# Zero rows below the low part of the filter states, so that the tap matmuls all have 128 rows

## The chip, the cores and the metric

The kernel runs on one core of one Trainium2 chip. The time is device microseconds of one execution; the number compared is the median over several executions. Lower is better.

## What is computed

One layer of a bidirectional encoder with 1024 tokens and 1024 channels in float32: an RMS norm, one input projection, a Hyena branch (512 channels, two long convolutions with implicit filters) beside windowed attention (8 heads), gates, norms, and an output projection with a residual. What matters here is how the filters come about and what they are used for:

```python
def hyena_filters(L, w1, b1, w2, b2, w3, b3, w4, sin_freq):
...
    h = jnp.sin(fr * (z @ w1.astype(F32) + b1.astype(F32)))
    h = jnp.sin(fr * (h @ w2.astype(F32) + b2.astype(F32)))
    h = jnp.sin(fr * (h @ w3.astype(F32) + b3.astype(F32)))
    h = (h @ w4.astype(F32)).reshape(L, HYENA_ORDER, N_DIRS, D_HYENA)
...
    return h * decay[:, None, None, :]

def long_conv(u, k_f, bias):
    L = u.shape[1]
    y = jnp.fft.irfft(jnp.fft.rfft(u, n=2 * L, axis=1) * k_f[None], n=2 * L, axis=1)[:, :L]
    return y + u * bias
```

The states h before w4 have 64 values for each of the 1024 positions (FILTER_HIDDEN is 64). The matmul with w4 makes the filter taps.

## The kernel before

All large matmuls run on float32 values that were split into a high part, rounded to the matmul's input type (F32R), and a low part, the rest. A product takes the terms high x high, high x low and low x high.

*The projection* goes through 26 column tiles of 128 channels. `weights` (L164 on) loads a tile by the SP queue into `wraw`, writes the high part on ACT, the negated high part in float32 on ACT into the low tile, and adds the raw weights onto it by a DMA of the POOL queue (L177). `half` (L192 on) makes the matmuls L198 to L200 with 512 columns each; `qkv_half` makes L285 to L287 with 256 columns.

*The Hyena branch* works on four quarters of 128 channels. A quarter has two long convolutions (`long_conv`: transform by matmuls L531, butterflies and products on VectorE, inverse transform by matmuls L570, product with a gate on VectorE, L571). Each needs the spectrum of its filter, made by `filter_spectrum`, eight calls in all. A call makes the taps in 8 chunks of 128 positions, two chunks to a PSUM bank: for each chunk L402 multiplies the high states `hh` with the weights, and L403 adds the low states `hl`. VectorE multiplies a bank with the decay (L404) into `eo`, and the transform matmuls L416 read `eo`. So there are 8 x 8 = 64 matmuls L402 and as many L403.

*How the taps' three terms fit two matmuls.* The contraction has only 64 values. `filter_weights` therefore stacks the weights in `wf`: rows 0 to 63 hold the high part, rows 64 to 127 the low part (L383, L384). `filter_mlp` writes the high states into both halves of `hh` (L359). One matmul of 128 rows, L402, gives high x high and high x low. L403 gives low x high with 64 rows, and its tile `hl` has 64 partitions (L354, written by L361).

*What sets the order.* The instructions are ordered when the program is built: `weave` runs the Hyena branch and the projection side by side, by costs that the generators yield, and a scheduler puts each engine's instructions into one order. TensorE thus works through taps, transforms and projections in a fixed sequence. Three PSUM banks (NF) serve the taps, the transforms and the inverse transforms.

Of the kernel before, what the change touches and what calls it, by code (L numbers as in the profile page):

```python
# [9 lines left out]
F32 = mybir.dt.float32  # L10
F32R = mybir.dt.float32r
I32 = mybir.dt.int32
AF = mybir.ActivationFunctionType
ALU = mybir.AluOpType
# [4 lines left out]
P = 128  # L19
S = 1024  # L20
# [24 lines left out]
def view(ap, off, dims):  # L45
    return bass.AP(
        tensor=ap.tensor, offset=ap.offset + off, ap=[list(ap.ap[0])] + [list(d) for d in dims]
    )


class Kernel:
# [268 lines left out]
    def filter_mlp(self, mp, keep, ps):  # L320
        nc, a = self.nc, self.a
        pk = mp.tile([P, 904], F32, name="mlp_in")
        nc.sync.dma_start(pk[:, 0:904], a["mlp_in"])
        yield
        zT, w1, fb = pk[0:66, 0:512], pk[0:66, 512:640], pk[:, 896:900]
        w23 = pk[:, 640:896].rearrange("p (l c) -> p l c", l=2)
        V = nc.vector
        h = None
        for l in range(3):
            pt = ps.tile([P, 512], F32, tag="g", name=self.nm("mlp"))  # L330
            if l == 0:
                nc.tensor.matmul(pt, w1, zT, start=True, stop=True)
            else:
                nc.tensor.matmul(pt, w23[:, l - 1, :], h, start=True, stop=True)
            y = mp.tile([P, 512], F32, tag="my", name=self.nm("my"))
            k = mp.tile([P, 512], F32, tag="mk", name=self.nm("mk"))
            V.tensor_scalar(
                out=y, in0=pt, scalar1=fb[:, l : l + 1], scalar2=fb[:, 3:4], op0=ALU.add, op1=ALU.mult
            )
            V.tensor_scalar(  # L340
                out=k, in0=y, scalar1=1.0 / (2.0 * math.pi), scalar2=MAGIC, op0=ALU.mult, op1=ALU.add
            )
            V.tensor_scalar(out=k, in0=k, scalar1=-MAGIC, scalar2=None, op0=ALU.add)
            V.scalar_tensor_tensor(out=y, in0=k, scalar=-TWO_PI_A, in1=y, op0=ALU.mult, op1=ALU.add)
            V.scalar_tensor_tensor(out=y, in0=k, scalar=-TWO_PI_B, in1=y, op0=ALU.mult, op1=ALU.add)
            V.tensor_scalar(
                out=y, in0=y, scalar1=3.1415925, scalar2=-3.1415925, op0=ALU.min, op1=ALU.max
            )
            h = mp.tile([P, 512], F32, tag="mh", name=self.nm("mh"), bufs=2)
            nc.scalar.activation(h, y, AF.Sin)  # L350
            yield

        hh = keep.tile([P, S], F32R, name="hh")
        hl = keep.tile([64, S], F32R, name="hl")  # L354
        self.hh, self.hl = hh, hl
        for n in range(2):
            cols, src = slice(512 * n, 512 * n + 512), h[64 * n : 64 * n + 64]
            for k in range(2):
                nc.scalar.copy(hh[64 * k : 64 * k + 64, cols], src)  # L359
            own = hh[64 * n : 64 * n + 64, cols]  # L360
            V.tensor_tensor(out=hl[:, cols], in0=src, in1=own.bitcast(F32), op=ALU.subtract)  # L361
        self.h3 = h

    def filter_weights(self, o, mp, keep, ps):
# [21 lines left out]
    def filter_spectrum(self, o, s, fp, ps):  # L386
        nc = self.nc
        V = nc.vector
        ADD, SUB = ALU.add, ALU.subtract
        if (o, s) == (0, 0):  # L390
            dec = self.dec0
        else:
            dec = self.dp.tile([P, 8, CH], F32, tag="dec", name=self.nm("dec"), bufs=1)
            nc.sync.dma_start(dec, self.a["decay"][s])
        eo = fp.tile([P, 8, 2, CH], F32, tag="eo", name=self.nm("eo"), bufs=1)
        wf = self.wf[:, o, s].rearrange("p e c -> p (e c)")
        for t in range(0, 8, 2):
            pt = ps.tile([P, 2, 2, CH], F32, tag="f", name=self.nm("gen"))
            for k in range(2):
                pf = pt[:, k].rearrange("p e c -> p (e c)")  # L400
                cols = slice((t + k) * P, (t + k + 1) * P)
                nc.tensor.matmul(pf, self.hh[:, cols], wf, start=True, stop=False)  # L402
                nc.tensor.matmul(pf, self.hl[:, cols], wf[0:64], start=False, stop=True)  # L403
            V.tensor_tensor(  # L404
                out=eo[:, t : t + 2], in0=pt, in1=view(dec[:, t], 0, [[CH, 2], [0, 2], [1, CH]]), op=ALU.mult
            )
            yield 1.1
        V.tensor_copy(eo[0:1, 0, 0, :], self.e0[32 * o : 32 * o + 1, s * CH : (s + 1) * CH])

        pos, neg = self.d, self.dn

        def dft(out, terms):
            for n, (m, t, e) in enumerate(terms):
                nc.tensor.matmul(out, m, eo[:, t, e], start=n == 0, stop=n == len(terms) - 1)  # L416

        def x_part(out, t):
            if t in (0, 4):
                dft(out[:, 0], [(pos[:, t, 0], t, 0)])  # L420
                dft(out[:, 1], [(pos[:, t, 1], t, 1)])
            else:
                dft(out[:, 0], [(pos[:, t, 0], t, 0), (pos[:, 8 - t, 0], 8 - t, 0)])
                dft(out[:, 1], [(pos[:, t, 1], t, 1), (pos[:, 8 - t, 1], 8 - t, 1)])

        def y_part(out, t):
            dft(out[:, 0], [(pos[:, t, 1], t, 0), (neg[:, 2 + t, :], 8 - t, 0)])
            dft(out[:, 1], [(neg[:, t - 1, :], t, 1), (pos[:, 8 - t, 0], 8 - t, 1)])

        def bank(a, b):  # L430
            pt = ps.tile([P, 2, 2, CH], F32, tag="f", name=self.nm("dft"))
            for k, (f, t) in enumerate((a, b)):
                f(pt[:, k], t)
            return pt

        def tmp(tag, n=2):
            return fp.tile([P, n, 2, CH], F32, tag=tag, name=self.nm(tag), bufs=1)

        def copied(pt):
            t = fp.tile([P, 2, 2, CH], F32, tag="c0", name=self.nm("fc"), bufs=2)  # L440
            nc.scalar.copy(t, pt)
            return t

        def tt(out, x, y, op):
            V.tensor_tensor(out=out, in0=x, in1=y, op=op)

        kt = fp.tile([P, 8, 2, CH], F32, tag="kt", name=self.nm("kt"), bufs=1)

        def two(q, r):
            return view(kt[:], q * 2 * CH, [[(r - q) * 2 * CH, 2], [1, 2 * CH]])  # L450

        flat = [[1, 2 * CH]]
        tq = tmp("t")
        x04 = copied(bank((x_part, 0), (x_part, 4)))
        tt(tq[:, 0], x04[:, 0], x04[:, 1], ADD)
        tt(tq[:, 1], x04[:, 0], x04[:, 1], SUB)
        xy2 = bank((x_part, 2), (y_part, 2))
        gh = fp.tile([P, 2, 2, 2, CH], F32, tag="b4", name=self.nm("gh"))
        tt(gh[:, 0], tq, xy2, ADD)
        tt(gh[:, 1], tq, xy2, SUB)  # L460
        yield 2.4
        xy1 = copied(bank((x_part, 1), (y_part, 1)))

        xy3 = bank((x_part, 3), (y_part, 3))
        uv = fp.tile([P, 2, 2, 2, CH], F32, tag="b4", name=self.nm("uv"))
        tt(uv[:, 0], xy1, xy3, ADD)
        tt(uv[:, 1], xy1, xy3, SUB)
        yield 1.4
        W = 2 * CH
        g01 = view(gh[:], 0, [[2 * W, 2]] + flat)  # L470
        h01 = view(gh[:], W, [[2 * W, 2]] + flat)
        uv0 = view(uv[:], 0, [[3 * W, 2]] + flat)
        tt(two(0, 2), g01, uv0, ADD)
        tt(two(4, 6), g01, uv0, SUB)
        uw = tmp("t")
        tt(uw[:, 0], uv[:, 1, 0], uv[:, 0, 1], ADD)
        tt(uw[:, 1], uv[:, 1, 0], uv[:, 0, 1], SUB)
        uwf = view(uw[:], 0, [[W, 2]] + flat)
        for q, r, c in ((1, 7, RT), (5, 3, -RT)):
            V.scalar_tensor_tensor(out=two(q, r), in0=uwf, scalar=c, in1=h01, op0=ALU.mult, op1=ADD)  # L480
        yield 3.2
        return kt
# [695 lines left out]
```

## Time and profile before

| | |
|---|---|
| median of 3 runs | 709.48 us (707.67 to 712.77) |
| the profiled execution | 707.97 us, its span 706.2 us |
| TensorE matmul busy | 660.3 us (94%) |
| VectorE busy | 527.4 us (75%) |
| ScalarE busy | 288.1 us (41%) |
| POOL busy | 56.5 us (8%) |
| mean granted TensorE clock | 0.978 |

Names in the profile: PE is TensorE's matmul, PEld its weight load, which runs beside matmuls, DVE is VectorE, ACT is ScalarE, POOL is GpSimd. A row such as `L403 PE MATMUL gen<-wf,hl 64*128 64x256 f32` tells the line, the engine, the output and inputs by tile names (buffer numbers left out), the loaded weights (rows * columns) and the moving operand (rows x columns). In rows in order of time the first number is the start in us from the start of the span, the second the length. Matmuls are pipelined: the start of the next one comes before the end of the last, and the distance between starts tells how long one holds the engine.

### The profile page before, as it was taken

To read this page: it belongs to the slowest core of one execution; us is meant where nothing else is said; L and a number is where in the kernel's file an instruction comes from. 1 tells how busy PE (TensorE), PEld (TensorE's weight loads), DVE (VectorE), ACT (ScalarE), POOL (GpSimd) and SP (SyncE) were. 2 spreads that over 40 slices of the span, in tenths; PEclk is the share of its full clock that TensorE was granted. 3 is DMA by queue.
4 is the path that set the end of the run, shared out by engine and by line. 5 is a ranking of instruction groups with operands and counts; after the bars stand their busy time and mean duration, and the time that the engine had idled before them with its cause. 6 is when DMAs were issued, how large, how long until landed. Compare 5 with 4: busy or idle time off the path is not lost.

```text
span 706.2 us, 10609 instructions
## 1 busy us (share of the span) xinstructions
PE 660.3 (94%) x3962; PEld 569.9 (81%) x3962; DVE 527.4 (75%) x1161; ACT 288.1 (41%) x549; POOL 56.5 (8%) x64
## 2 busy tenths in 40 slices
PE   1489999999799999999999999999899899999997
PEld 1357788998788999888889888778787788988886
DVE  3878699598696998978979869444688878876422
ACT  6455343225242322432332423587377634343210
POOL 1341000001010000110100101010000000000000
PEclk9989999999999999999999999999899789999999
DMA  8934644235544313762450546754434731222331
GB/s 281 255 90 90 194 107 102 91 74 135 169 113 127 73 47 135 174 138 77 115 184 31 117 138 149 221 157 120 134 130 128 262 123 59 97 91 98 111 107 59
DMA packets 46888, 90.13 MB, mean 128 GB/s; under 512 B 7154, under 2 KB 15986, under 8 KB 46580
## 3 DMA queue, kind: packets, MB, share of 16 engines
q1 hardware_dynamic: 36656, 73.22, 31.3%
q0 software_dynamic: 7488, 13.63, 11.3%
q10 hardware_dynamic: 2692, 2.60, 1.3%
q8 instruction: 31, 0.51, 0.3%
q14 instruction: 21, 0.17, 0.1%
HBM read 53.78 MB, written 22.02 MB: 107 GB/s over the span
## 4 chain that ended last, share of the span: by engine, by line
PE 80%; DMA 13%; DVE 3%; ACT 2%; issue 2%; SPq 0%; ACTq 0%; DVEq 0%; POOLq 0%
PE proj L198 9%; PE proj L200 9%; PE proj L199 8%; PE pv L757 5%; PE dft L416 5%; PE fw L531 4%; PE inv L570 4%; PE po L844 4%; PE po L845 4%; PE po L846 4%; PE qkv L287 3%; PE qkv L285 3%; PE qkv L286 3%; DMA w_lo<-wraw 3%; PE gen L403 3%; PE gen L402 2%
## 5 line engine op out<-in xcount | busy, mean ns | idle before, releaser
L199 PE MATMUL proj<-h,w_hi 128*128 128x512 f32 x320 | 130.1, 407 | 1.8 <-DVE h L160 1.2
L198 PE MATMUL proj<-h,w_hi 128*128 128x512 f32 x320 | 129.1, 404 | 2.8 <-ACT h L158 2.8
L200 PE MATMUL proj<-h,w_lo 128*128 128x512 f32 x320 | 128.3, 401 | 0.0
L177 POOL DMA_DIRECT2D w_lo<-wraw x52 | 45.0, 866 | 418.8 <-ACT w_lo L176 383.4
L199 PEld LDWEIGHTS proj<-h,w_hi 128*128 128x128 f32 x320 | 61.1, 191 | 17.1 <-DVE h L160 2.4
L198 PEld LDWEIGHTS proj<-h,w_hi 128*128 128x128 f32 x320 | 61.2, 192 | 15.3 <-ACT h L158 3.6
L200 PEld LDWEIGHTS proj<-h,w_lo 128*128 128x128 f32 x320 | 61.3, 191 | 13.4 <-issue 1.3
L174 ACT CAST w_hi<-wraw 128x512 fp32r<-128x512 f32 x52 | 32.2, 620 | 76.1 <-DMA wraw<-in_w_in 39.6
L287 PE MATMUL qkv<-w_hi,h 128*128 128x256 f32 x192 | 54.9, 286 | 0.0
L285 PE MATMUL qkv<-w_hi,h 128*128 128x256 f32 x192 | 54.8, 286 | 0.0
L286 PE MATMUL qkv<-w_lo,h 128*128 128x256 f32 x192 | 54.8, 286 | 0.0
L757 PEld LDWEIGHTS pv<-vv,pf 128*128 128x128 f32 x352 | 49.5, 205 | 2.4 <-PE bT L719 0.2
L757 PE MATMUL pv<-vv,pf 128*128 128x66 f32 x352 | 48.7, 282 | 0.0
L416 PE MATMUL dft<-eo,d 128*128 128x128 f32 x352 | 46.8, 276 | 0.0
L416 PEld LDWEIGHTS dft<-eo,d 128*128 128x128 f32 x352 | 43.4, 192 | 0.6
L706 DVE CUSTOM_DVE_ANT_0 mj<-smax,mask 128x384 f32<-128x384 f32 (+1 forms) x64 | 33.4, 522 | 13.9 <-PE smax L701 10.8
L287 PEld LDWEIGHTS qkv<-w_hi,h 128*128 128x128 f32 x192 | 36.9, 192 | 0.5
L286 PEld LDWEIGHTS qkv<-w_lo,h 128*128 128x128 f32 x192 | 36.9, 192 | 0.2
L285 PEld LDWEIGHTS qkv<-w_hi,h 128*128 128x128 f32 x192 | 36.9, 192 | 0.3
L176 ACT ACTIVATE w_lo<-wraw 128x512 fp32r<-128x512 f32 x52 | 32.7, 629 | 10.5 <-PE qkv L286 10.5
L743 ACT ACTIVATE pf<-st 128x768 f32<-128x768 f32 (+1 forms) x32 | 24.2, 756 | 29.6 <-DVE st L741 26.8
L531 PE MATMUL fw<-u,d 128*128 128x128 f32 x256 | 33.4, 285 | 2.4 <-DMA u<-hy 2.3
(196 smaller groups left out, 1439.7 us busy)
## 6 DMA issues: line engine op xcount, KB each, us to landing
wraw<-in_w_in SPq DMA_DIRECT2D x52, 256.0 KB, 3.0
w_lo<-wraw POOLq DMA_DIRECT2D x52, 256.0 KB, 3.6
hy<-hraw SPq DMA_DIRECT2D x12, 512.0 KB, 2.6
x<-in_x_t SPq DMA_DIRECT2D x8, 512.0 KB, 5.4
dec<-in_decay SPq DMA_DIRECT2D x8, 512.0 KB, 3.9
g<-hy SPq DMA_DIRECT2D x8, 512.0 KB, 3.9
gt<-graw SPq DMA_DIRECT2D x16, 256.0 KB, 3.7
woraw<-in_w_out SPq DMA_DIRECT2D x16, 256.0 KB, 3.2
```

The source lines that it names most:

```text
L176: nc.scalar.mul(l, raw, -1.0)
L177: nc.gpsimd.dma_start(l.bitcast(F32), raw, accum_op=ALU.add)
L198: nc.tensor.matmul(pt, hi[:, k], xh, start=k == 0, stop=False)
L199: nc.tensor.matmul(pt, hi[:, k], xl, start=False, stop=False)
L200: nc.tensor.matmul(pt, lo[:, k], xh, start=False, stop=k == 7)
L285: nc.tensor.matmul(pt[:, b], hh, hi[:, :, k], start=k == 0, stop=False)
L286: nc.tensor.matmul(pt[:, b], hh, lo[:, :, k], start=False, stop=False)
L287: nc.tensor.matmul(pt[:, b], hl, hi[:, :, k], start=False, stop=k == 7)
L416: nc.tensor.matmul(out, m, eo[:, t, e], start=n == 0, stop=n == len(terms) - 1)
L531: nc.tensor.matmul(pt[:, k, c], self.d[:, t + k, c], u[:, t + k], start=True, stop=True)
L706: V.tensor_tensor_reduce(out=junk[:, 0:nk], in0=pm[:, 0:nk], in1=mask, op0=ALU.add, op1=ALU.max, scale=1.0, scalar=NEG, accum_out=mx[:, 4 ...
L757: nc.tensor.matmul(pv[:, h], probs[:, n, cols], self.vv[:, k0 + n, g], start=n == 0, stop=n == nk - 1)
```

## The change

The tile `hl` gets 128 partitions. Its partitions 64 to 127 are set to zero once, on GpSimd, and the low states are written into partitions 0 to 63, as before. L403 (L404 in the changed kernel) then reads all 128 rows of `hl` and all 128 rows of `wf`. What it adds is the same: the low states meet the high weights, and the zeros meet the low weights. In the matmul, `hl` is the operand that is loaded, `wf` the one that moves.

```diff
         hh = keep.tile([P, S], F32R, name="hh")
-        hl = keep.tile([64, S], F32R, name="hl")
+        hl = keep.tile([P, S], F32R, name="hl")
+        nc.gpsimd.memset(hl[64:128].bitcast(F32), 0.0)
         self.hh, self.hl = hh, hl
...
-            V.tensor_tensor(out=hl[:, cols], in0=src, in1=own.bitcast(F32), op=ALU.subtract)
+            V.tensor_tensor(out=hl[0:64, cols], in0=src, in1=own.bitcast(F32), op=ALU.subtract)
...
                 nc.tensor.matmul(pf, self.hh[:, cols], wf, start=True, stop=False)
-                nc.tensor.matmul(pf, self.hl[:, cols], wf[0:64], start=False, stop=True)
+                nc.tensor.matmul(pf, self.hl[:, cols], wf, start=False, stop=True)
```

The order of TensorE, VectorE, ScalarE and SP stays the same, instruction by instruction. POOL gets one more. This is the head of POOL's order before (the four constants are the program's own, `w_lo` the low weights of the projection, `wraw` what was loaded for them):

```order
L1168 MEMSET const-float32-0.0 128x1
L1168 MEMSET const-float32-1.0 128x1
L1168 MEMSET const-bfloat16-1.0 128x1
L1168 MEMSET const-uint8-127 128x1
L1174 UNCONDITIONAL_BRANCH
L177 DMA w_lo<-wraw_150 128x512
L177 DMA w_lo<-wraw_155 128x512
```

And the same place now:

```order
L1169 MEMSET const-float32-0.0 128x1
L1169 MEMSET const-float32-1.0 128x1
L1169 MEMSET const-bfloat16-1.0 128x1
L1169 MEMSET const-uint8-127 128x1
L1175 UNCONDITIONAL_BRANCH
L355 MEMSET hl 64x1024
L177 DMA w_lo<-wraw_150 128x512
L177 DMA w_lo<-wraw_155 128x512
```

The memset stands ahead of POOL's first DMA for the projection's weights; the rest of POOL's order follows as before.

On TensorE this is how taps stand among projections (here the first chunks of the second spectrum, `gen`, with the inverse transform of the convolution before, `inv`, ahead of them and the projection `qkv` behind). Before:

```order
L570 MATMUL inv_742<-V_713,di 128x128 x2
L402 MATMUL gen_755<-wf,hh 128x256
L403 MATMUL gen_755<-wf,hl 128x256
L402 MATMUL gen_755<-wf,hh 128x256
L403 MATMUL gen_755<-wf,hl 128x256
L287 MATMUL qkv_1163<-w_hi,h_89 128x256
```

And now, one line number further on:

```order
L571 MATMUL inv_743<-V_714,di 128x128 x2
L403 MATMUL gen_756<-wf,hh 128x256
L404 MATMUL gen_756<-wf,hl 128x256
L403 MATMUL gen_756<-wf,hh 128x256
L404 MATMUL gen_756<-wf,hl 128x256
L287 MATMUL qkv_1164<-w_hi,h_89 128x256
```

Nothing moved there; the rows tell the size of the output, which is the same, and not the rows of the operands, which are what changes.

## What I predicted, before the changed kernel ran

> **What bounds the kernel now.** I read the page first, for the chain that ended last, then the waits of TensorE and VectorE in the stretch where filter taps are made, then single rows there.
>
> From the page: the profiled span, and the chain by engine.
>
> ```profile
> span 706.2 us, 10609 instructions
> PE 80%; DMA 13%; DVE 3%; ACT 2%; issue 2%; SPq 0%; ACTq 0%; DVEq 0%; POOLq 0%
> ```
>
> The taps are made between 68 and 412 us. First TensorE's waits between 66 and 455 us (total, times, longest), then VectorE's waits between 114 and 412 us, where seven of the eight spectra lie, and the busy time of that stretch (length, then PE, PEld, DVE, ACT, POOL, the granted clock, the DMA share).
>
> ```profile
> PE uT L230 <- DVE hsc L220: 3.9, 1, 3.9
> PE fw L531 <- DMA u<-hy: 2.3, 2, 1.5
> DVE eo L404 <- PE gen L403: 13.2, 18, 1.6
> DVE u L571 <- PE inv L570: 7.0, 7, 1.8
> 114.00:412.00 298.00, 292.59 (x1911) 260.12 (x1911) 251.87 (x439) 95.71 (x190) 24.81 (x29) 0.99 0.42 115
> ```
>
> TensorE waits three times in 389 us, 6.2 us in all. It sets the pace here, and what leaves it can leave the time. But VectorE is busy 251.87 of 298 us (85%), so it comes next: 46 us of slack. The two of its waits that lie among the taps are for the taps themselves (13.2) and for the inverse transform that runs between them (7.0).
>
> **What a 64-row matmul costs.** The groups by shape (mean ns of one last before the bar; matmuls overlap, so a mean is no cost), then TensorE in order of time: one pair of tap chunks among projections, two neighbours of an earlier one, plain 256-column matmuls, and the 66-row matmuls of the attention.
>
> ```profile
> L403 PE MATMUL gen<-wf,hl 64*128 64x256 f32 x64 | 23.9, 378 | 0.0
> L286 PE MATMUL qkv<-w_lo,h 128*128 128x256 f32 x192 | 54.8, 286 | 0.0
> L736 PE MATMUL st<-qb,kt 66*128 66x256 f32 x88 | 25.0, 304 | 0.8 <-ACT qb L721 0.8
> ...
> 77.44 0.39 PE L200 MATMUL proj<-h,w_lo 128*128 128x512 f32 x1
> 77.67 0.28 PE L402 MATMUL gen<-wf,hh 128*128 128x256 f32 x1
> 77.88 0.38 PE L403 MATMUL gen<-wf,hl 64*128 64x256 f32 x1
> 78.19 0.38 PE L402 MATMUL gen<-wf,hh 128*128 128x256 f32 x1
> 78.50 0.38 PE L403 MATMUL gen<-wf,hl 64*128 64x256 f32 x1
> 78.81 0.50 PE L198 MATMUL proj<-h,w_hi 128*128 128x512 f32 x1
> 79.15 0.39 PE L199 MATMUL proj<-h,w_hi 128*128 128x512 f32 x1
> ...
> 68.57 0.50 PE L403 MATMUL gen<-wf,hl 64*128 64x256 f32 x2
> ...
> 113.94 0.28 PE L285 MATMUL qkv<-w_hi,h 128*128 128x256 f32 x1
> 114.06 0.28 PE L286 MATMUL qkv<-w_lo,h 128*128 128x256 f32 x1
> 114.17 0.28 PE L287 MATMUL qkv<-w_hi,h 128*128 128x256 f32 x1
> ...
> 476.53 0.29 PE L736 MATMUL st<-qb,kt 66*128 66x256 f32 x1
> 476.65 0.28 PE L735 MATMUL st<-qa,kt 128*128 128x256 f32 x1
> 476.77 0.28 PE L736 MATMUL st<-qb,kt 66*128 66x256 f32 x1
> ```
>
> Read the distances between starts. Plain 256-column matmuls follow each other in 0.12 us. L402 to L403 and back takes 0.31, and the 512-column L198 behind the last L403 takes 0.34. Without a 64-row neighbour a 512-column one takes 77.67 - 77.44 = 0.23. Each matmul loads its own weights, so a new load alone is not what costs: the plain ones load too. Nor is it short rows as such: 66 rows and 128 rows alternate in the attention at 0.12. What is left is the change between a 64-row and a 128-row shape, either way.
>
> From 77.44 to 79.15 are 1.71 us; two matmuls of 512 columns and four of 256 at the plain pace are 2 x 0.23 + 4 x 0.12 = 0.94. The excess is 0.77 for two L403, thus 0.385 each, two switches of 0.19.
>
> **The change part by part.**
>
> *The matmuls.* All 64 L403 become 128-row matmuls of the same 256 columns, and nothing else on TensorE changes. Price of one afterwards: at best the 0.12 of L286, at worst what it is now (0.31). I take 0.12, since L286 has the very shape (128*128, 256 columns) and L402, its neighbour, already has it. That a product with zeros is slower no row suggests. The gain on TensorE is 64 x 0.385 = 24.6, less four switches (0.8) in the first spectrum, where two L403 stand together (the x2 row at 68.57, and one more such pair) and share them: 24 us (3.4% of the span).
>
> The Trainium skill ("TensorE: Matmul & The Clock Gate", Part 3, The mechanism) says that weight loads overlap matmuls in flight only when their row groups differ. By that rule a 128-row load behind a 128-row matmul could not overlap, and the gain would be nil, a time of 708. The rows at 113.94 to 114.17 speak against it.
>
> *The larger tile.* The tile has 4 KB in a partition as before. L361 writes the same 64 rows.
>
> *The memset.* It is POOL's first work. Its price lies between the kernel's 128x1 memset and twice POOL's 128x512 subtraction (1024 elements a partition instead of 512).
>
> ```profile
> 0.24 0.10 POOL L1168 MEMSET const-float32-0.0<- 128x1 f32 x1 [0.24 <-issue]
> 11.99 1.90 POOL L177 DMA_DIRECT2D w_lo<-wraw  x2 [11.54 <-ACT w_lo L176]
> 28.15 1.39 POOL L160 TENSOR_TENSOR h<-x,h 128x512 fp32r<-128x512 f32 x1
> ```
>
> That is 0.1 to 2.8 us, and I take 2.8, the nearer size. POOL is idle for 11.54 us before its first DMA, so it costs nothing on the path; without that cover it would delay the w_lo DMA by those 2.8. The first reader, L403, comes at 68.57. No other engine waits for it before.
>
> **How much of the 24 us arrives.** *First spectrum (66 to 87).* The chain leaves TensorE here (start, length; the row at 369.89 is for the clock, below), and one VectorE row shows what stands before e0p:
>
> ```profile
> 73.24 0.95 PE e0p L378 x2
> 75.97 7.09 DMA hy<-hraw
> 83.14 3.52 DMA u<-hy
> 86.79 1.14 PE fw L531 x8
> ...
> 369.89 2.47 PE fw L531 x20
> ...
> 71.92 1.28 DVE L382 TENSOR_TENSOR wd<-w 64x512 f32<-64x512 f32 x2 [2.07 <-DMA w<-in_filt_w]
> ```
>
> Eight L403 save 8 x 0.385 - 0.8 = 2.3 us there, 0.8 of it at 77.44, after the store of hy began. The second e0p needs the weights whose landing released L382 at 71.92, so it can move from 73.2 by about 1.2 at most. I take 1.2 (ends 0 and 2.3). The rest becomes a longer wait for u, which is late next.
>
> *The seven others.* On TensorE each has 8 L403 x 0.385 = 3.08 us. The next transform needs the taps after VectorE's multiplication with the decay, so a spectrum cannot shrink by more than VectorE's own waits in it. Those are 13.2 + 7.0 = 20.2 us over the seven. In two of them they are more than TensorE can give (the seventh, then the eighth):
>
> ```profile
> DVE eo L404 <- PE gen L403: 2.4, 2, 1.6
> DVE u L571 <- PE inv L570: 1.6, 1, 1.6
> ...
> DVE u L571 <- PE inv L570: 2.4, 2, 1.8
> DVE eo L404 <- PE gen L403: 1.5, 3, 0.6
> ```
>
> 4.0 and 3.9 count as 3.08 each, so 20.2 - 0.9 - 0.8 = 18.5 us. The remaining 3 us of TensorE's gain turn into short waits for eo in front of the transforms. The ends are 10 (only half comes through, since VectorE is 85% busy and a late eo delays the next step) and 21.6 (7 x 3.08).
>
> *The clock.* After TensorE's longest wait (3.9 us, for hsc) the granted clock fell. After the 1.5 us wait for u, which ended at 369.89, it did not. Later there was a stretch at half (500 to 505).
>
> ```profile
> 184.10:188.00 3.90, 3.88 (x20) 3.90 (x21) 3.28 (x7) 1.17 (x2) 0.00 (x0) 0.56 0.08 24
> 369.90:374.00 4.10, 4.10 (x37) 4.10 (x38) 3.28 (x8) 1.48 (x3) 0.00 (x0) 1.00 0.01 5
> 500.00:505.00 5.00, 5.00 (x21) 4.44 (x21) 4.54 (x6) 4.13 (x5) 0.00 (x0) 0.50 0.13 52
> ```
>
> Such a stretch costs 3.9 x 0.44 = 1.7 us. The two waits for u, at 86.79 (2.3 - 1.5 = 0.8 us now) and at 369.89, may reach 2 us. I take 1.0 for both together (ends 0 and 3.4).
>
> *Sum.* -1.2 - 18.5 + 1.0 = -18.7. The profiled execution took 707.97 us, its span and 1.8 around it, so 689.3. The median before is 709.48, 1.5 above that execution; for a median I put half of that on top: 690.
>
> **Rivals.**
> 1. *All of it arrives*: TensorE is the only bound, and VectorE's work moves into its 46 us of slack. 708 - 24 = 684. For it: three waits in 389 us. Against it: 85% busy, and the single eo waits are smaller than what TensorE saves.
> 2. *VectorE takes the pace*: only half of the seven spectra's gain and none of the first: 708 - 10 = 698. For it: VectorE must do the same eo and u work in order, with its other steps between. Against it: its waits all end at TensorE.
> 3. *No change*: the 0.31 stays, because it belongs to two matmuls that add into one bank, or because the weight load of L403 is not hidden with 128 rows either (where the page's rule above would lead). The gain is 0, the time 708 to 709.5. Against it: L285 to L287 add into one bank at 0.12 with loads of 128 rows, and the plain L198 behind L403 pays too.
> 4. *Slower*: the new short waits drop the clock at every spectrum and at the two waits for u, in longer stretches. At ten places, each 5 us at 0.50, that loses 2.5 us, 25 in all: 708 - 18.7 + 25 = 714. It decides from eight places on. Against it: 1.00 after the 1.5 us wait. The Trainium skill ("TensorE: Matmul & The Clock Gate", Why this matters for your kernels) puts the limit at idle gaps of about 3 us; by that rule these waits cost nothing, and the time is 688. The row from 369.90 agrees.
>
> **How the numbers follow.** My forecast has 0.70, rivals 1 to 4 have 0.10, 0.14, 0.04 and 0.02. The range runs from rival 1 (684) to rival 2 (698) and leaves out under 2 in 10. A measurement can tell about 1% from no change, that is 702.4 here: the forecast and rivals 1 and 2 lie below, so faster 0.94, same 0.04, slower 0.02.
>
> **What would show it.** Right: L403's successor (L404 in the changed kernel) reads 128*128, and a pair of chunks among projections takes 0.94 us instead of 1.71; VectorE's waits for gen in the seven spectra fall from 13.2 to a few us; TensorE shows new waits for eo under 1 us; the stretch from 114 to 412 takes some 18 us less with the same 252 us of VectorE in it. The forecast is wrong where starts stay 0.31 apart (rival 3), where waits of TensorE for VectorE add up to over 10 us (rival 2), or where the clock row shows more half-speed stretches (rival 4).

## The result, and the profile after

The changed kernel takes 688.82 us (median of 4 runs, 686.11 to 691.81), against 709.50 us for the kernel before (4 runs, 707.67 to 712.77). The ratio is 0.9705, with a 95% interval from 0.9642 to 0.9767. The forecast was 690.0 us, with a range from 684 to 698.

The profiled execution after is the fastest of the four, 686.11 us, 21.9 us below the profiled execution before. From its page: the span, the busy time of the engines, and the chain that ended last.

```profile
span 684.3 us, 10610 instructions
PE 634.8 (93%) x3962; PEld 559.3 (82%) x3962; DVE 525.5 (77%) x1161; ACT 287.8 (42%) x549; POOL 57.0 (8%) x65
PE 74%; DMA 15%; ACT 3%; issue 3%; DVE 3%; POOL 1%; SPq 0%; POOLq 0%; DVEq 0%; ACTq 0%
```

TensorE is 25.5 us less busy (660.3 before), and all other engines have practically the same work. TensorE's share of the chain fell from 80 to 74%, and that of DMAs rose from 13 to 15%. So TensorE still bounds the kernel, but a little more of the time is set by transfers.

Now the place that the prediction priced: TensorE in order of time (start, length), the same two pairs of tap chunks among projections.

```profile
74.91 0.39 PE L200 MATMUL proj<-h,w_lo 128*128 128x512 f32 x1
75.14 0.28 PE L403 MATMUL gen<-wf,hh 128*128 128x256 f32 x1
75.26 0.28 PE L404 MATMUL gen<-wf,hl 128*128 128x256 f32 x1
75.38 0.28 PE L403 MATMUL gen<-wf,hh 128*128 128x256 f32 x1
75.50 0.28 PE L404 MATMUL gen<-wf,hl 128*128 128x256 f32 x1
75.61 0.39 PE L198 MATMUL proj<-h,w_hi 128*128 128x512 f32 x1
75.84 0.39 PE L199 MATMUL proj<-h,w_hi 128*128 128x512 f32 x1
```

Read the starts again. Every step between two tap matmuls is 0.11 to 0.12 us, and the 512-column matmul behind them takes 0.23, as it does elsewhere. From the first row to the last are 0.93 us; before they were 1.71.

Then the waits: TensorE's between 66 and 460 us, and below them VectorE's and the busy times of the stretch from 112.5 to 391.8 us. That stretch holds the same 1911 TensorE matmuls as 114 to 412 us before.

```profile
PE uT L230 <- DVE hsc L220: 5.5, 1, 5.5
PE fw L532 <- DMA u<-hy: 3.5, 3, 2.6
PE kT L679 <- ACT kk L670: 1.8, 1, 1.8
```

```profile
DVE u L572 <- PE inv L571: 3.1, 5, 1.1
DVE eo L405 <- PE gen L404: 0.5, 1, 0.5
```

```profile
112.50:391.80 279.30, 272.88 (x1911) 253.89 (x1909) 249.90 (x439) 94.31 (x188) 24.07 (x28) 0.99 0.43 118
```

The stretch is 298.0 - 279.3 = 18.7 us shorter with nearly the same VectorE work in it. VectorE's idle time in it fell from 46.1 to 29.4 us. Its waits for taps fell from 13.2 to 0.5, and those for the inverse transform from 7.0 to 3.1. TensorE's waits for `hsc` and u grew from 6.2 to 9.0 us together, and no wait for `eo` over 0.15 us came in.

Where the time went is plainest from the starts of the same TensorE instruction in both executions. "Saved" is the start before less the start after, in us:

| filter spectrum | first tap matmul | first transform of the taps (L416, L417) | first transform of u (L531, L532) |
|---|---|---|---|
| 1 | 1.30 | 3.31 | 1.48 |
| 2 | 1.52 | 4.28 | 4.28 |
| 3 | 4.28 | 7.37 | 4.98 |
| 4 | 4.64 | 7.67 | 7.67 |
| 5 | 7.69 | 10.55 | 10.56 |
| 6 | 10.56 | 13.47 | 13.47 |
| 7 | 13.49 | 15.98 | 17.18 |
| 8 | 17.18 | 20.19 | 20.19 |

Behind the table it is 19.1 from 464 us on (the wait for `kk`, 0.7 before, is 1.8), 22.1 from 509 us on, and 21.84 at the end. The 1.30 us ahead of the first tap do not come from the change: no instruction before it differs but the memset, and with the memset alone (below) the first tap starts 1.14 us earlier than in the profile before, too.

A table from single executions is only as good as those, and that of the changed kernel is the fastest of its three profiles. From the first to the eighth transform of u it saves 20.19 - 1.48 = 18.7 us; the profiles of two repeats of the changed kernel (below) save 16.4 and 16.5 us there against the same profile before.

### The profile page after: what moved, and what is told of

It is laid out like the page before. It is cut to its first block, busy times and chain, and to the rows that moved or that the text cites. A ratio compares the mean times of both kernels' runs of the same rounds, so it can differ in the third digit from the quotient of the medians.

```text
span 684.3 us, 10610 instructions
## 1 busy us (share of the span) xinstructions
PE 634.8 (93%) x3962; PEld 559.3 (82%) x3962; DVE 525.5 (77%) x1161; ACT 287.8 (42%) x549; POOL 57.0 (8%) x65
## 4 chain that ended last, share of the span: by engine, by line
PE 74%; DMA 15%; ACT 3%; issue 3%; DVE 3%; POOL 1%; SPq 0%; POOLq 0%; DVEq 0%; ACTq 0%
PE proj L199 8%; PE proj L198 8%; PE proj L200 8%; PE pv L758 5%; PE fw L532 5%; PE dft L417 5%; PE po L845 4%; PE po L846 4%; PE po L847 4%; DMA w_lo<-wraw 4%; PE inv L571 4%; PE qkv L285 3%; PE qkv L286 3%; PE qkv L287 3%; DMA wraw<-in_w_in 2%
## 5 line engine op out<-in xcount | busy, mean ns | idle before, releaser
L199 PE MATMUL proj<-h,w_hi 128*128 128x512 f32 x320 | 128.8, 402 | 1.8 <-DVE h L160 1.0
L198 PE MATMUL proj<-h,w_hi 128*128 128x512 f32 x320 | 127.4, 399 | 2.9 <-ACT h L158 2.9
L200 PE MATMUL proj<-h,w_lo 128*128 128x512 f32 x320 | 126.9, 396 | 0.0
L200 PEld LDWEIGHTS proj<-h,w_lo 128*128 128x128 f32 x320 | 60.8, 190 | 12.3 <-issue 1.0
L286 PE MATMUL qkv<-w_lo,h 128*128 128x256 f32 x192 | 54.6, 284 | 0.0
L417 PE MATMUL dft<-eo,d 128*128 128x128 f32 x352 | 46.6, 275 | 0.0
L417 PEld LDWEIGHTS dft<-eo,d 128*128 128x128 f32 x352 | 43.4, 192 | 0.4
L532 PE MATMUL fw<-u,d 128*128 128x128 f32 x256 | 33.7, 286 | 3.6 <-DMA u<-hy 3.5
L286 PEld LDWEIGHTS qkv<-w_lo,h 128*128 128x128 f32 x192 | 36.8, 192 | 0.1
```

The source lines that it names most:

```text
L198: nc.tensor.matmul(pt, hi[:, k], xh, start=k == 0, stop=False)
L199: nc.tensor.matmul(pt, hi[:, k], xl, start=False, stop=False)
L200: nc.tensor.matmul(pt, lo[:, k], xh, start=False, stop=k == 7)
L286: nc.tensor.matmul(pt[:, b], hh, lo[:, :, k], start=False, stop=False)
L532: nc.tensor.matmul(pt[:, k, c], self.d[:, t + k, c], u[:, t + k], start=True, stop=True)
```

## The experiments

Each experiment was compared with runs of the kernel before on the same chip. The first three ask what the price was and what removed it; the others ask where the third spectrum's gain went. The first four ran on one chip beside the kernel before at 711.48 us (13 runs).

| kernel | median us (lowest to highest, runs) | ratio to before (95%) |
|---|---|---|
| half the switches | 698.23 (697.59 to 699.89, 4) | 0.9813 (0.9793 to 0.9833) |
| 96 rows | 690.69 (689.63 to 692.13, 4) | 0.9705 (0.9685 to 0.9725) |
| memset only | 711.82 (706.70 to 715.91, 10) | 1.0018 (0.9987 to 1.0049) |
| two tables | 687.47 (684.49 to 689.55, 4) | 0.9655 (0.9623 to 0.9688) |
| changed kernel again | 690.90 (690.53 to 697.79, 4) | 0.9738 (0.9676 to 0.9801) |
| u early | 687.59 (685.61 to 690.09, 4) | 0.9671 (0.9612 to 0.9729) |
| one table | 693.19 (690.89 to 695.31, 4) | 0.9747 (0.9697 to 0.9797) |
| table and u | 686.75 (684.17 to 687.03, 4) | 0.9649 (0.9603 to 0.9695) |
| changed kernel, third time | 688.68 (685.34 to 694.23, 6) | 0.9682 (0.9645 to 0.9719) |
| table and u, more rounds | 686.07 (683.78 to 691.33, 6) | 0.9667 (0.9623 to 0.9712) |

The fifth to eighth kernels ran beside the kernel before at 709.21 us (7 runs), the last two beside 709.62 (10 runs).

### Half the switches

The kernel before, with the 64-row matmul kept. In the second chunk of each bank the low part comes first, so that two 64-row matmuls stand together and share their switches.

```diff
-                nc.tensor.matmul(pf, self.hh[:, cols], wf, start=True, stop=False)
-                nc.tensor.matmul(pf, self.hl[:, cols], wf[0:64], start=False, stop=True)
+                parts = [(self.hh, wf), (self.hl, wf[0:64])]
+                for n, (x, y) in enumerate(parts if k == 0 else parts[::-1]):
+                    nc.tensor.matmul(pf, x[:, cols], y, start=n == 0, stop=n == 1)
```

> The 64-row low parts are kept; in each bank the second chunk takes its low part first (high, low, low, high), so that two 64-row matmuls stand together: 2 changes of shape in a bank instead of 4, 64 in all instead of 128. Theory (each change between 64 and 128 rows costs 0.19 us of TensorE): 32 banks x 2 x 0.19 = 12.3 us less on TensorE, 9 to 12 us less in time, a ratio to before of about 0.985; from one low part to the next 0.12 us. Rival (a 64-row matmul costs 0.385 us more wherever it stands): no change, ratio 1.00. Rival (two matmuls adding into one bank cost it): no change either.

Measured: 13.2 us less than the kernel before (711.48 - 698.23), ratio 0.9813. That is 1 us more than the 9 to 12 expected, and the runs do not show where it comes from. TensorE in order of time at the same place (start, length; all taps are line L404 here):

```profile
75.68 0.39 PE L200 MATMUL proj<-h,w_lo 128*128 128x512 f32 x1
75.90 0.28 PE L404 MATMUL gen<-wf,hh 128*128 128x256 f32 x1
76.11 0.50 PE L404 MATMUL gen<-wf,hl 64*128 64x256 f32 x2
76.54 0.39 PE L404 MATMUL gen<-wf,hh 128*128 128x256 f32 x1
76.77 0.40 PE L198 MATMUL proj<-h,w_hi 128*128 128x512 f32 x1
```

Against the plain 0.12 a matmul, the one ahead of the pair takes 0.21 (76.11 - 75.90), the two 64-row ones 0.43 together instead of 0.24, and the one behind 0.23. The excess is 0.09 + 0.19 + 0.11 = 0.39 us for two changes of shape, half of the 0.77 that four changes cost before, with as many 64-row matmuls. So the price belongs to the change of shape and not to the 64-row matmul. One expectation missed: from one low part to the next it is 0.22 us and not 0.12, because half of a change's price falls on the matmul behind it.

Summed over all stretches of tap matmuls and the one instruction behind each, what exceeds the plain pace (0.12, and 0.23 for 512 columns) is 24.9 us before, 14.1 us here and 2.4 us in the changed kernel. Most of those 2.4 us come with other neighbours: a tap matmul right behind a 128-column one takes 0.20 us in the changed kernel as well. So the changes of shape cost 22.5 us in all, and half of them 11.7. Each bank still has two matmuls adding into one place, so adding into the same bank is not the cause either.

### 96 rows

The changed kernel with 96 instead of 128 rows for the low part: 64 rows of states and 32 of zeros.

```diff
-        hl = keep.tile([P, S], F32R, name="hl")
-        nc.gpsimd.memset(hl[64:128].bitcast(F32), 0.0)
+        hl = keep.tile([96, S], F32R, name="hl")
+        nc.gpsimd.memset(hl[64:96].bitcast(F32), 0.0)
...
-                nc.tensor.matmul(pf, self.hl[:, cols], wf, start=False, stop=True)
+                nc.tensor.matmul(pf, self.hl[:, cols], wf[0:96], start=False, stop=True)
```

> The low part gets 96 rows: 64 of data, 32 of zeros (the weights' low parts of those rows meet zeros). Theory (only 64 rows or fewer make the other shape): as with 128 rows, 0.12 us between starts of tap matmuls, ratio 0.965 to 0.975. Rival (any change of the row count costs 0.19 us): starts stay 0.31 us apart, ratio 1.00. Rival (cost falls with the rows): between, ratio about 0.985.

Measured: 690.69 us, ratio 0.9705, the ratio of the changed kernel. Again TensorE in order of time:

```profile
75.03 0.28 PE L403 MATMUL gen<-wf,hh 128*128 128x256 f32 x1
75.15 0.28 PE L404 MATMUL gen<-wf,hl 96*128 96x256 f32 x1
75.27 0.28 PE L403 MATMUL gen<-wf,hh 128*128 128x256 f32 x1
75.39 0.28 PE L404 MATMUL gen<-wf,hl 96*128 96x256 f32 x1
```

Shapes of 96*128 and 128*128 alternate at 0.12 us. Equal row counts are thus not needed. 64 rows pay beside 128; 96 do not, and neither do the attention's 66.

### The memset alone

The kernel before with the larger tile and the memset, while the matmul still reads 64 rows.

```diff
+        hl = keep.tile([P, S], F32R, name="hl")
+        nc.gpsimd.memset(hl[64:128].bitcast(F32), 0.0)
...
-                nc.tensor.matmul(pf, self.hl[:, cols], wf[0:64], start=False, stop=True)
+                nc.tensor.matmul(pf, self.hl[0:64, cols], wf[0:64], start=False, stop=True)
```

> The larger tile and the memset alone; the matmul still reads 64 rows. Theory: the memset is hidden by GpSimd's 10 us of idle time at the start, ratio 1.00 within 0.3%. Rival (the memset or the tile's place is part of the gain or costs something): ratio off 1.00 by more than that.

Measured: 711.82 us over 10 runs, ratio 1.0018 (0.9987 to 1.0049). The tile and the memset cost nothing that can be measured, and bring nothing. The gain is the matmuls' shape alone.

### Two tables

In the changed kernel TensorE's longest wait, in the third spectrum, grew from 3.9 to 5.5 us (to 6.6 and 7.2 us in its two repeats). It waits for `hsc` on VectorE, which stands behind L261, a product with a table that a DMA has not yet brought. VectorE, then TensorE, of the changed kernel in order of time (in brackets the idle time before, and what ended it):

```profile
176.63 0.42 DVE L261 TENSOR_TENSOR tab<-tab,gq 128x256 f32<-128x256 f32 x1 [3.02 <-DMA tab<-in_rope]
176.97 1.28 DVE L220 SCALAR_TENSOR_TENSOR hsc<-hraw,conv_w,hsc 128x1023 f32<-128x1023 f32 x1
...
178.40 1.73 PE L230 MATMUL uT<-ident,hsc 128*128 128x128 f32 x7 [5.51 <-DVE hsc L220]
```

The edit gives the table a second buffer, so that its load can start earlier (a tile of ones is cut to one column to make room).

```diff
-        self.ones = cp.tile([P, P], F32, name="ones")
+        self.ones = cp.tile([P, 1], F32, name="ones")
...
-        tab = ap.tile([P, 2, 4, 64], F32, tag="tab", name=self.nm("tab"))
+        tab = ap.tile([P, 2, 4, 64], F32, tag="tab", name=self.nm("tab"), bufs=2)
```

> The changed kernel with a second buffer for the rotary table (space for it from a tile of ones that is cut to the one column that is read), so that the table's load can go out before the old table is used up. Theory (the third spectrum's gain was lost because VectorE's convolution step stood behind the table's product, which waited for that load): TensorE's wait of 5.5 us for hsc goes, and with it the half clock behind it; 2 to 6 us less than the changed kernel, ratio to before 0.962 to 0.968. Rival (the load of u behind the store of the old one holds the next transform at the same time anyway): TensorE's wait goes over to u, the time stays that of the changed kernel, ratio 0.970.

Measured: 687.47 us, ratio 0.9655, and the wait stayed. VectorE and TensorE in order of time:

```profile
181.10 0.43 DVE L261 TENSOR_TENSOR tab<-tab,gq 128x256 f32<-128x256 f32 x1 [4.03 <-DMA tab<-in_rope]
...
182.87 1.73 PE L230 MATMUL uT<-ident,hsc 128*128 128x128 f32 x7 [6.54 <-DVE hsc L220]
```

The second buffer moved an earlier load forward, and another table load then stood at this place. The edit did not take away what it was meant to, so it tells nothing about the wait's worth, and that the time lies in the range that was expected for a wait that goes is no support. The order of TensorE's instructions behind 297 us changed with it as well.

### u early, one table, and both

Two things are late in the third spectrum: the table for VectorE, and u, whose load stands behind the store of the quarter before. The chain of the changed kernel in order of time (start, length) shows the second:

```profile
169.89 4.37 DMA zd<-u
...
174.34 5.88 DMA u<-hy
...
180.35 5.32 PE fw L532 x32
```

The transform of u could start at 180.35 at the earliest, whatever the wait for `hsc`. Three edits of the changed kernel, with the changed kernel itself beside them.

*u early* writes the second result of a quarter into the gate's tile, so that u's buffer is free before the store:

```diff
-            V.tensor_tensor(out=out[:, t : t + 4], in0=pt, in1=gate[:, t : t + 4], op=MUL)
+            dst = gate if out is None else out
+            V.tensor_tensor(out=dst[:, t : t + 4], in0=pt, in1=gate[:, t : t + 4], op=MUL)
...
+        return gate
...
-        z2 = rows("u", 1)
-        yield from self.long_conv(kt, z, stored(2, "g", 1), z2, bp, ps)
+        z2 = yield from self.long_conv(kt, z, stored(2, "g", 1), None, bp, ps)
```

> The changed kernel with the second convolution's result written into its gate's tile, so that the next quarter's u can be loaded before that result is stored. Theory (the third spectrum lost its gain to the rotary table's load alone): TensorE's wait for hsc near 178 stays, the time is that of the changed kernel or up to 2 us less. Rival (the store and load of u hold the transform there): that wait falls by 2 us or more and the time by 3 to 5 us.

*One table* loads the table of each kind once and keeps it (it also has the second buffer and the smaller tile of ones from above, left out here):

```diff
-        tab = self.rope_table(p // 2, half, ap)
+        if p // 2 not in self.tabs:
+            self.tabs[p // 2] = self.rope_table(p // 2, half, ap)
+        tab = self.tabs[p // 2]
```

> The changed kernel with the rotary table for queries loaded once, early, into a second buffer, instead of twice behind the work that uses it (the tile of ones is cut to its one column for the space). This takes the table's load out of the place near 175 us altogether. Theory (VectorE's convolution step behind the table's product is what TensorE waits for): the wait of 5.5 us for hsc goes; the next transform still waits for u until about 180, so 2 to 5 us less than the changed kernel, most of it from the half-clock stretch that no longer follows. Rival (u alone sets the time there): a wait of the same length for u takes its place, the time stays within 1 us.

*Table and u* has both edits:

> Both of these together: the table loaded once and early, and u loaded before the store. Theory (two loads, each hidden behind the other, hold TensorE near 178): only now does the whole wait go, with 5 to 9 us less than the changed kernel, a ratio to before of 0.958 to 0.963. Rival (the projection's weights, which arrive late on ScalarE there, hold it too): no more than the better of the two alone.

*The changed kernel again*, unedited:

> The changed kernel once more, beside the three that follow. Theory: ratio to before 0.965 to 0.975, the same waits of TensorE at u (2.6 us near 85), hsc (5.5 us near 178) and the same half-clock stretch behind the latter.

Measured: 687.59 for u early, 693.19 for one table, 686.75 for both, 690.90 for the changed kernel again. Each of the three intervals overlaps with that of the changed kernel. One table was expected to be 2 to 5 us faster and came out 2.3 us slower; both together were expected to gain 5 to 9 us, and 4.2 us is less. The traces tell more than the times. TensorE's longest waits between 66 and 460 us, first of u early:

```profile
PE fw L532 <- DVE uv L446: 5.4, 1, 5.4
PE inv L571 <- DVE V L506: 3.0, 1, 3.0
```

Of one table:

```profile
PE fw L535 <- DVE t L449: 6.0, 1, 6.0
PE fw L535 <- DMA u<-hy: 2.6, 2, 1.8
```

Of both (the first row's wait ends at 438.5 us, behind the last spectrum):

```profile
PE kT L683 <- ACT kk L674: 2.1, 1, 2.1
PE fw L535 <- DMA u<-hy: 2.0, 1, 2.0
PE dft L420 <- ACT fc L445: 1.1, 1, 1.1
```

Each edit alone takes the wait for `hsc` away and leaves one of the same size at the same place. With u early it is 5.4 us for VectorE's `uv`, which stands behind the same table product (near 298 us comes another 3.0 us, for `V`). With one table it is 6.0 us, which the profile puts down to VectorE's `t`. But the transform reads u and not `t`, and u landed at 179.92 us, 0.02 us before `t` was done:

```profile
176.19 0.33 SPq L589 DMA_DIRECT2D u<-hy  x1
179.18 0.75 DVE L449 TENSOR_TENSOR t<-uv 128x256 f32<-128x256 f32 x2
180.06 5.88 PE L535 MATMUL fw<-u,d 128*128 128x128 f32 x32 [6.00 <-DVE t L449]
```

So it is the load of u that held TensorE there, as the rival of that experiment said. Only both edits together remove the wait; 0.4 and 0.9 us are left. The edits also changed TensorE's order at this place: in all three the transform of u stands ahead of the transposes `uT` that wait for `hsc`, and in the changed kernel behind them. What this order does to the waits is not separated from what the loads do.

With both edits TensorE ran 3 to 5 us ahead of the changed kernel's fastest execution until 380 us, and by 446 us that lead was gone; against the two repeats of the changed kernel, 2.5 and 3.6 us of it were left. A half-clock stretch from 439.6 to 443 us lies there, and the wait for `kk` is 0.3 us longer; that these are all of it is not shown.

### The changed kernel and both edits, once more

> The changed kernel a third time, in more rounds, as the partner of the next one. Theory: ratio to before 0.968 to 0.975, about 689 to 691 us.

> The kernel with both the table loaded once and u loaded early, in more rounds. Theory (the wait near 178 was worth some microseconds, part of which come back later as the wait for the first keys): 2 to 5 us less than the changed kernel beside it, the two intervals apart or nearly so. Rival (all of it is taken back behind 440 us): the two medians within 1 us.

Measured: 688.68 us (6 runs) against 686.07 (6 runs), ratios 0.9682 (0.9645 to 0.9719) and 0.9667 (0.9623 to 0.9712). The version with both edits was 4.2 us and 2.6 us below the changed kernel in the two comparisons, and the intervals overlap both times. Whether it is faster is not settled.

## Why the prediction was right, and where its steps were not

**The price of a switch: right.** The prediction put 0.385 us on each L403, two switches of 0.19, and 24 us on all. The pair of chunks fell from 1.71 to 0.93 us (0.94 predicted), and the excess summed over all taps from 24.9 to 2.4 us, thus by 22.5 of the 24. That it is the change of shape, as the prediction argued from the attention's 66 rows, is shown from two more sides: half the switches left 11.7 of the 22.5 us, and 96 rows cost nothing.

**Rival 3, no change: excluded.** The group of the changed L404 (all 64; busy time and mean ns of one behind the bar):

```profile
L404 PE MATMUL gen<-wf,hl 128*128 128x256 f32 x64 | 16.8, 288 | 0.0
```

Its mean fell from 378 to 288 ns, which is L286's 286. The Trainium skill ("TensorE: Matmul & The Clock Gate", Part 3, The mechanism) says in its list of what overlaps that a weight load overlaps matmuls in flight only when the row groups differ. This trace disagrees with that sentence: from 75.14 to 75.61 four matmuls, each with a load of 128 rows, pass in 0.47 us. Another page of the Trainium skill, "TensorEngine Tiling (Array Packing)", Key Properties, says that a change of the tiling mode drains TensorE. It gives no price; the rows here fit it with 0.19 us for a change between 64 and 128 rows. That these 64-row matmuls run in such a mode no run shows.

**The memset: hidden, and smaller than assumed.** POOL in order of time:

```profile
0.74 0.95 POOL L355 MEMSET hl<- 64x1024 f32 x1 [0.29 <-POOLq L1169]
11.94 1.90 POOL L177 DMA_DIRECT2D w_lo<-wraw  x2 [10.25 <-ACT w_lo L176]
```

It took 0.95 us where 2.8 was assumed, and POOL was idle for 10.25 us behind it. The experiment with the memset alone gives a ratio of 1.0018.

**The first spectrum: 0.2 us of 1.2 in this profile, more against another.** Predicted were 1.2 us; 1.48 - 1.30 = 0.2 arrived. The second `e0p` did move by the step that the prediction took: its start, 73.17 before, is 70.64 now, 2.53 earlier, 1.30 of them from ahead of the taps, so 1.2 from the change. The chain in order of time shows what became of it:

```profile
73.85 7.03 DMA hy<-hraw
80.96 4.21 DMA u<-hy
```

The store of hy began 75.97 - 73.85 = 2.12 us earlier, thus 0.8 by the change and not 1.2: the copies of `hraw` on ScalarE were held by another cast just before. Then the load of u took 4.21 us instead of 3.52. That is not shown to be the change's work. The memset alone has the old matmuls, and its load of u was as long:

```profile
82.06 4.22 DMA u<-hy
```

So the short load is that of one execution of the kernel before. From the first tap matmul to the first transform of u the changed kernel is 0.95 us shorter than the memset alone (its repeats 1.3 and 1.2), close to the 1.2 predicted.

TensorE had its transform of the taps 3.31 us earlier and gave 1.8 of it back in the wait for u:

```profile
85.30 1.13 PE L532 MATMUL fw<-u,d 128*128 128x128 f32 x8 [2.59 <-DMA u<-hy]
```

That wait was 0.77 before (1.43 with the memset alone) and 2.2 us in both repeats; "a longer wait for u, which is late next" was right, and its size larger than thought.

**The seven others: the sum near, its parts not.** Predicted were 18.5 us; the table gives 18.7. That it is so close is luck in part, since the two repeats give 16.4 and 16.5. And the prediction held that a spectrum cannot shrink by more than VectorE's own waits in it: 4.0 and 3.9 us in the last two, and 12.3 in the other five, 2.5 each. Measured, second to eighth, from the first transform of u to the next: 2.80, 0.70, 2.69, 2.89, 2.91, 3.71, 3.01. The second, fourth, fifth and sixth gained more than 2.5, near TensorE's own 3.08. The seventh's 3.71 holds 0.9 us of a wait for u that was shorter this time (0.68 instead of 1.53). The third gained 3.09 at its taps (7.37 - 4.28) and lost 2.4 behind them.

Why the cap did not hold can be seen at the end of the taps. The kernel before, in order of time, VectorE's last multiplication and TensorE's first transform in the third spectrum:

```profile
172.21 0.69 DVE L404 TENSOR_TENSOR eo<-gen,dec 128x512 f32<-128x512 f32 x1 [0.79 <-PE gen L403]
172.44 0.61 PE L416 MATMUL dft<-eo,d 128*128 128x128 f32 x4
```

And the changed kernel, where one row stands for three multiplications without a gap:

```profile
163.90 1.88 DVE L405 TENSOR_TENSOR eo<-gen,dec 128x512 f32<-128x512 f32 x3
165.07 0.61 PE L417 MATMUL dft<-eo,d 128*128 128x128 f32 x4
```

In both the transform starts before VectorE has multiplied the last bank (done at 172.90 and 165.78). It reads chunks 0 and 4 first and those of the last bank, 6 and 7, behind them, so it does not wait for VectorE to be done. VectorE can thus fall a bank behind TensorE there and catch up in its other idle time; no experiment tests this reading by itself. The same rows answer rival 2: VectorE's idle time fell by 16.7 us, it waits for taps once instead of 18 times, and TensorE does not wait for it.

What the third spectrum lost is the part of the sum that was missing. TensorE reached the place 7.4 us earlier than before, but the table's load went out only 4.7 us earlier (at 169.96 instead of 174.69). TensorE's wait grew by 1.6 us, from 3.9 to 5.5, and the stretch at half clock around it was 6.8 us long (176.7 to 183.5) instead of 3.4. Both repeats have 6.8 us there too, and the memset alone 3.4. This is its window behind the wait (the granted clock is the third number from the end):

```profile
178.40:183.60 5.20, 4.97 (x22) 4.60 (x23) 3.25 (x7) 1.17 (x2) 0.00 (x0) 0.51 0.27 98
```

The three edits show that two late things hold TensorE here, the table and u, and that taking one away leaves the other.

**The clock: the feared stretch came in two of three profiles.** The prediction added 1.0 us for the two waits for u. They became 2.59 and about 0.7 us, the first over the 2 us that the prediction feared, and in this execution no half-clock stretch followed either. In both repeats one followed the first of them, a wait of 2.2 us that ended at 85.31 and 86.83 us. This is the window in the first repeat (the second is at half from 87.1 to 90.5):

```profile
86.30:89.70 3.40, 3.40 (x19) 3.40 (x18) 0.88 (x3) 0.73 (x2) 0.00 (x0) 0.50 0.00 0
```

It costs 3.4 x 0.5 = 1.7 us, and from the first to the second transform of u the repeats saved 1.43 us each where the table has 2.80. The limit of about 3 us that the prediction took from the Trainium skill ("TensorE: Matmul & The Clock Gate", Why this matters for your kernels) did not hold in these two. So the prediction's term was there for a reason, and its absence in the profiled execution was luck. The longer stretch around the wait for `hsc` the prediction had not foreseen. Against it, a stretch of the kernel before is absent here. The clock windows at the same work, before and after:

```profile
498.60:505.40 6.80, 6.42 (x27) 5.70 (x26) 5.26 (x8) 5.11 (x7) 0.00 (x0) 0.50 0.26 83
```

```profile
476.50:483.30 6.80, 4.94 (x35) 4.29 (x36) 5.39 (x6) 2.70 (x4) 0.00 (x0) 1.00 0.32 93
```

That is the step from 19.2 to 22.1 us saved between 498.6 and 505.4 us. It is not the change's work: in the repeats of the changed kernel there was half clock from 482.2 to 485.6 and from 483.0 to 489.9 us. In the same way the 1.30 us ahead of the first tap go with a half-clock stretch at 48 to 55 us in the profile before; the memset alone has none there and gained 1.14 us of them. Without these two, the profiled difference of 21.8 us is 0.2 + 18.7 - 1.1 (the wait for `kk`) = 17.8 us from the change, 0.9 less than the predicted 18.7. The same sum for the two repeats is 15.9 and 16.2. The median of 688.82 us lies 1.2 below the predicted 690.0; that the forecast is so near is thus partly luck, since the half-clock stretches that come and go are as large as what it missed.

**Rivals 1 and 4.** All of it arriving would have given 684 us. What kept about 6 of the 24 us away: 1.8 at u in the first spectrum, 2.4 in the third, 1.1 at `kk` (with the memset alone that wait was 1.5 us, so part of the 1.1 may be chance), and what VectorE and single waits took in the others. Rival 4 asked for half clock at eight places; after the change there is one such place among the taps in this profile, and two in each repeat.

## What to carry to other kernels

Read the distances between starts on TensorE rather than mean durations, and look for matmuls whose loaded rows alternate between 64 and 128: here each change of shape cost 0.19 us, and zero rows, which cost nothing themselves, took the price away; standing equal shapes next to each other takes half of it. Of the time saved on the engine that sets the pace, nearly all arrived here where its only partner was an engine with slack, and little where the next step hung on a transfer. Where a long wait is held by two late things, taking one away changes the name in the trace and not the wait. And one profile is one execution: a second one of the same kernel, or of an edit that changes nothing, tells which of its differences are the change's.

## What the runs showed of the hardware that was not expected

The price of a change of shape, 0.19 us, is spread over both sides: about 0.1 us on the matmul ahead of it and as much on the one behind, be that one of 256 columns (0.23 instead of 0.12) or of 512 (0.34 instead of 0.23). It appears between 64 and 128 rows, and not between 66 or 96 and 128.

GpSimd set 64x1024 float32 elements to zero in 0.95 us, about 1.1 elements in a nanosecond for each partition.

Some half-clock stretches come in every profile, others come and go. The one at the wait for `hsc` was there in all profiles of the kernel before, the memset alone and the changed kernel. Near 500 us of the kernel before, the same instructions had 6.8 us of half clock in one execution, 3.4 us in another and none in a third; and a wait of 2.2 us for u was followed by one in both repeats, while 2.24 us with 96 rows and 2.59 us in the first profile were not. From 60 us to the last microseconds, every such stretch in these profiles lasted 3.4, 6.8, 10.2, 13.7 or 17.1 us, a multiple of 3.4. In the profiles of the changed kernel the mean granted clock was 0.985, 0.979 and 0.972, with spans of 684.3, 688.8 and 692.5 us. That is as large as the effects of the last experiments, which is why what u early, one table and both are worth stays open.
